# Gathered rows of the expert layer given in portions among the keys of its dense stage

## The chip, the cores and the metric

One core of a Trainium2 chip runs the whole program as one launch. The metric is the device time of the launch in microseconds, the median of several runs. The core's engines each have a queue that is worked off in order: TensorE (PE), VectorE (DVE), ScalarE (ACT), GpSimd (POOL) and SyncE (SP), which here only starts transfers.

## What is computed

A decoder block on 1024 tokens of width 1024: a time mixing and an attention run side by side and are merged, and behind them stands an expert layer. Only that layer is touched. For each token and each of 8 heads it scores 128 + 128 sub-keys, keeps the 16 best pairs, and so gets 128 expert numbers (of 16384) with a gate each:

```python
ids = (e1 * PK_NKEYS + e2).reshape(T, PK_HEADS * PK_TOPK)
gates = jax.nn.softmax(vals, axis=-1).reshape(T, PK_HEADS * PK_TOPK)
def chunk(args):                       # 128 tokens
    xc, idc, gc = args
    act = jnp.einsum('ced,cd->ce', u_tab[idc], xc)
    act = jax.nn.gelu(act, approximate=False) * gc
    return jnp.einsum('ce,ced->cd', act, v_tab[idc])
```

The sum is added to the block's input, and a last norm gives the output. All in float32.

## The kernel before

The tokens are taken in two groups of 512. For each group `mix` does the mixing part and `pick` the sub-key scores; `choose` then makes the expert numbers and gates of 128 tokens. The expert layer is done in two ways.

The first 512 tokens, four blocks of 128, go the **gathered** way (`peer`, L823). For each of the 128 chosen experts of a block, `gather` (L807) has GpSimd start an indirect transfer that brings one row of the table u for each token, 128 x 1024 numbers, into one of five buffers (tile `uv`); VectorE multiplies it with the tokens and sums (L831). Then a Gelu and the gate, and the same with 128 rows of v, which VectorE adds up with their weights (L838). `finish` (L813) squares on ScalarE, loads the weight row of the last norm, normalises on VectorE (L820) and stores. So there are 1024 gathered rows in all, each one transfer on the software queue and one VectorE operation.

The last 512 tokens go the **dense** way (`dense`, L877): all 16384 experts are worked off, 128 at a time, for all 512 tokens together. One such portion of experts is a key e, from 0 to 127. `head(e)` (L891) gets the products of the tokens with u (`dots`: two loads on SP into `wraw`, split into a high and a low part on ScalarE at L177 and VectorE at L178, 24 matmuls at L192 to L196), takes Gelu (L899), multiplies with the gates (L901, once for each key: it serves as the marker of a key below), and splits the result (`ah`, `al`, L199 and L200) and the two loaded halves of v (`vraw`, L907, to `vh` and `vl`). `add` (L912) then has 3 matmuls for each of six banks that stay in place over all keys; two more outputs are summed over two keys at a time and evicted (`rest`, L921 and L923). For the first 16 keys (NE) the products with u are made ahead, while the gates are scattered into their dense form (`gates`). At the end the banks are added (L942) and four blocks finished, with two buffers for the weight row.

The order of each engine's queue is made when the program is built: a planner goes through its own estimate of time and gives each engine the operation that is ready, the one that stands earlier in the program's text first. So text order is a rank among ready operations. In the old text the four calls of `peer` stand behind the whole of `dense`. `head(e + 1)` stands ahead of the matmuls of key e.

Of the kernel before, what the change touches and what calls it, by code (L numbers as in the profile page):

```python
# [18 lines left out]
P = 128  # L19
D = 1024  # L20
T = 1024
# [6 lines left out]
NA = 10  # L28
N4 = 4
NU = 5  # L30
ND = 4
NB = 5
NW = 3
# [15 lines left out]
def body(ctx: ExitStack, tc: tile.TileContext, ins, out, dbg=None):  # L49
# [10 lines left out]
    def zbank(name):  # L60
        return ps.tile([P, 512], F32, name=name, tag="zb", bufs=2)
# [16 lines left out]
    def at(name, dt=F32):  # L78
        return hp.tile([P, 512], dt, name=name, tag="at", bufs=NA)
# [4 lines left out]
    def t4(name):  # L84
        return hp.tile([P, D], F32, name=name, tag="t4", bufs=N4)
# [112 lines left out]
    def split(src, hi, lo):  # L198
        nc.scalar.activation(hi, src, AF.Copy)  # L199
        nc.vector.tensor_tensor(lo, src, hi.bitcast(F32), op=OP.subtract)  # L200

    def mm3(o, ah, al, bh, bl, first, last):
        nc.tensor.matmul(o, ah, bh, start=first, stop=False)  # L203
        nc.tensor.matmul(o, ah, bl, start=False, stop=False)  # L204
        nc.tensor.matmul(o, al, bh, start=False, stop=last)  # L205
# [23 lines left out]
    def normed(src, w):  # L229

        xn = [rt("xn") for _ in HALVES]
        ssq = tiny("ssq", 2)
        for i in range(2):
            nc.scalar.activation(xn[i], src[i], AF.Square, accum_out=ssq[:, i:i + 1])
        r = invroot(ssq[:, 0:1], 1, 1.0 / D, 1e-6, more=ssq[:, 1:2])
        for i in range(2):
            nc.vector.scalar_tensor_tensor(xn[i], src[i], r[:, 0:1], w[i], op0=OP.mult, op1=OP.mult)
        return xn
# [27 lines left out]
    def mix(gi, t0, W, xin=None):  # L266
# [414 lines left out]
        for a in range(TT):  # L681
# [6 lines left out]
            hn = normed(xs, nw)  # L688
            if t0 + a * P < T - ND * P:
                for i, c in enumerate(HALVES):  # L690
# [4 lines left out]
    def pick(t0, W, fh, fl):  # L695
# [5 lines left out]
        for hc in range(16):  # L701
# [12 lines left out]
            for a in range(TT):  # L714
# [7 lines left out]
                nc.vector.max_index(ix[:, 8:16], v[:, 8:16], s2)  # L722
        return [(v1[a], i1[a], t0 // P + a, t0 + a * P >= T - ND * P) for a in range(TT)]

# [82 lines left out]
    def gather(src, ids, j):  # L807
        t = pp_.tile([P, D], F32, name="uv", bufs=NU)
        nc.gpsimd.indirect_dma_start(out=t, out_offset=None, in_=ins[src],  # L809
                                     in_offset=bass.IndirectOffsetOnAxis(ap=ids[:, j:j + 1], axis=0))  # L810
        return t

    def finish(acc, rows, pool, tag, bufs):  # L813

        ssq = pool.tile([P, 1], F32, name="ssqf", bufs=2)
        fnw = pool.tile([P, D], F32, name="fnw", tag=tag, bufs=bufs)
        nc.scalar.activation(fnw, acc, AF.Square, accum_out=ssq)
        nc.sync.dma_start(fnw, ins["fnw"].to_broadcast([P, D]))
        r = invroot(ssq, 1, 1.0 / D, 1e-6, pool=pool)
        nc.vector.scalar_tensor_tensor(acc, acc, r[:, 0:1], fnw, op0=OP.mult, op1=OP.mult)  # L820
        nc.sync.dma_start(out[rows, :], acc)

    def peer(bi, ids, gate):  # L823

        rows = slice(bi * P, (bi + 1) * P)
        act = pp_.tile([P, P], F32, name="act", bufs=2)
        hb = pp_.tile([P, D], F32, name="hb", tag="ha", bufs=2)
        nc.sync.dma_start(hb, ins["hfs"][rows, :])
        for j in range(P):
            u = gather("u", ids, j)  # L830
            nc.vector.scalar_tensor_tensor(u, u, 1.0, hb, op0=OP.mult, op1=OP.mult, accum_out=act[:, j:j + 1])  # L831
        nc.scalar.activation(act, act, AF.Gelu)
        nc.vector.tensor_tensor(act, act, gate, op=OP.mult)
        acc = pp_.tile([P, D], F32, name="acc", tag="ha", bufs=2)
        nc.sync.dma_start(acc, ins["x1s"][rows, :])
        for j in range(P):
            v = gather("v", ids, j)
            nc.vector.scalar_tensor_tensor(acc, v, act[:, j:j + 1], acc, op0=OP.mult, op1=OP.add)  # L838
        finish(acc, rows, pp_, "uv", NU)

    def gates(sp, a, sl, eye8):

# [22 lines left out]
    def dots(e, W, fh, fl):  # L865
        b = zbank("ua")[:, :W]
        wmul(b, ins["ut"][e], lambda k: fh[:, k, :W], lambda k: fl[:, k, :W], step=8)
        return b
# [8 lines left out]
    def dense(t0, W, fh, fl):  # L877

        TT = W // P
        fp = ctx.enter_context(tc.tile_pool(name="fp", bufs=1))  # L880
        acc = []
        for a in range(TT):
            acc.append(t4("accd"))
            nc.sync.dma_start(acc[a], ins["x1s"][t0 + a * P:t0 + (a + 1) * P, :])
        outs = [(a, 0) for a in range(TT)] + [(a, 1) for a in range(TT)][::-1]
        banks = (rbank, rbank, rbank, obank, abank, abank)
        kept = {o: f("yk") for o, f in zip(outs, banks)}
        moved = outs[len(banks):]
        gt = [None]

        def head(e):  # L891

            if e % CE == 0:
                gt[0] = fp.tile([P, 512 // QT, CE, QT], F32, name="gt", bufs=2)
                nc.sync.dma_start(gt[0][:, :W // QT], ins["gd_s"][e // CE, :, 0:W // QT])
            w = fp.tile([P, 512], F32, name="gw", bufs=2)[:, :W]
            if e < NE:
                nc.sync.dma_start(w, ins["a_s"][e, :, 0:W])
            nc.scalar.activation(w, w if e < NE else dots(e, W, fh, fl), AF.Gelu)  # L899
            w3 = w.rearrange("p (q t) -> p q t", t=QT)  # L900
            nc.vector.tensor_tensor(w3, w3, gt[0][:, :W // QT, e % CE, :], op=OP.mult)  # L901
            v = []
            ah, al = at("ah", F32R)[:, :W], at("al", F32R)[:, :W]
            split(w, ah, al)
            for h, c in enumerate(HALVES):
                raw = fp.tile([P, 512], F32, name="vraw", bufs=NVR)
                nc.sync.dma_start(raw, ins["v"][e * P:(e + 1) * P, c])  # L907
                v.append([fp.tile([P, 512], F32R, name=n, tag=f"v{h}", bufs=NV[h]) for n in ("vh", "vl")])
                split(raw, *v[h])
            return ah, al, v  # L910

        def add(o, b, r, first, last):  # L912
            ts = slice(o[0] * P, (o[0] + 1) * P)
            mm3(b, r[0][:, ts], r[1][:, ts], *r[2][o[1]], first, last)

        def rest(o, rs):
            b = zbank("yr")
            for i, r in enumerate(rs):
                add(o, b, r, i == 0, i == CV - 1)
            t = fp.tile([P, 512], F32, name="ye", bufs=2)  # L920
            nc.scalar.activation(t, b, AF.Copy)  # L921
            y = acc[o[0]][:, HALVES[1]]
            nc.vector.tensor_tensor(y, y, t, op=OP.add)  # L923

        rs = [head(0)]
        for e in range(P):
            nxt = head(e + 1) if e + 1 < P else None
            full = rs[:CV] if e % CV == 0 and e else None
            if full:
                rs = rs[CV:]  # L930
            for n, (o, b) in enumerate(kept.items()):
                if full and n in MV:
                    rest(moved[MV.index(n)], full)
                add(o, b, rs[-1], e == 0, e == P - 1)
            rs.append(nxt)
        for o in moved:
            rest(o, rs[:CV])
        for a in range(TT):
            for h in range(2):
                if (a, h) in kept:  # L940
                    y = acc[a][:, HALVES[h]]
                    nc.vector.tensor_tensor(y, y, kept[a, h], op=OP.add)  # L942
            finish(acc[a], slice(t0 + a * P, t0 + (a + 1) * P), fp, "gt", 2)

    todo, late = [], []
# [11 lines left out]
    if "nopeer" not in dbg:  # L957
        with tc.tile_pool(name="sp", bufs=1) as sp:
            eye_f = sp.tile([P, P * 8], F32, name="eye_f", bufs=1)
            nc.sync.dma_start(eye_f, ins["eye8"])  # L960
            eye8 = sp.tile([P, P, 8], BF, name="eye8", bufs=1)
            nc.vector.tensor_copy(eye8.rearrange("p e t -> p (e t)"), eye_f)
            o = W - ND * P
            fh, fl = fh[:, :, o:W], fl[:, :, o:W]
            for a, c in enumerate(late[o // P:]):
                gates(sp, a, choose(*c), eye8)
                ahead(sp, ND * P, fh, fl, range(a * NE // ND, (a + 1) * NE // ND))
            todo += [(c[2], *choose(*c)) for c in late[:o // P]]
        dense(t0 + o, ND * P, fh, fl)
        for t in todo:  # L970
            peer(*t)


def prepare(inputs):
# [72 lines left out]
```

## Time and profile before

| | us |
|---|---|
| median of 3 runs | 3443.16 (3440.47 to 3446.24) |
| the profiled execution | 3435.12 |
| its span | 3433.4 |
| mean granted TensorE clock | 0.941 of full speed |

The profile is of one execution. Its span is what lies between the first and the last instruction; the execution is 1.7 us longer, and 8.0 us shorter than the median of the runs. Busy shares are of time; a busy DMA share is the mean of the core's 16 DMA engines.

### The profile page before, as it was taken

Reading aid. Unit: us, or ns where it says so; the run is one execution under the profiler, and the core shown is the slowest. Engines: PE = TensorE matmul, PEld = TensorE weight load, DVE = VectorE, ACT = ScalarE, POOL = GpSimd, SP = SyncE. Lnnn points to the kernel's source line nnn. Section 1 sums busy time; section 2 is a strip of 40 time slices with the busy share of each in tenths; the row PEclk is TensorE's granted clock in tenths of the full one; section 3 lists DMA queues with packets and bytes.
Section 4 is the critical chain, followed back from the end, with each engine's and each line's share of the span. In section 5 each row is a group of like instructions: output and inputs, shape, how many; then the busy total and the mean of one; then the engine's idle time right before and its main releaser. Section 6 shows DMA issues by size and latency. Waiting matters only on the chain.

```text
span 3433.4 us, 50842 instructions
## 1 busy us (share of the span) xinstructions
PE 3041.2 (89%) x17382; PEld 2379.3 (69%) x17382; DVE 2855.4 (83%) x6337; ACT 1410.6 (41%) x2632; POOL 1328.8 (39%) x1037
## 2 busy tenths in 40 slices
PE   7999998989988878798887689999998999898992
PEld 5777777766766656576565568777777777676872
DVE  5565548989898789998887689998989999889997
ACT  4444424434434423239998333333323333333331
POOL 0000000054533454212124256655655665655664
PEclk9999999999999889899988799999999999999996
DMA  4222444276666788656769999999999999999997
GB/s 135 81 77 74 140 152 161 81 253 209 216 217 222 274 322 314 204 164 187 234 202 324 333 321 353 362 348 353 355 365 350 359 354 355 360 358 350 350 327 275
DMA packets 407525, 898.68 MB, mean 262 GB/s; under 512 B 69025, under 2 KB 140001, under 8 KB 403169
## 3 DMA queue, kind: packets, MB, share of 16 engines
q0 software_dynamic: 147456, 536.94, 43.8%
q1 hardware_dynamic: 259808, 358.49, 31.2%
q8 instruction: 137, 2.24, 0.3%
q14 instruction: 124, 1.01, 0.1%
HBM read 829.22 MB, written 66.07 MB: 261 GB/s over the span
## 4 chain that ended last, share of the span: by engine, by line
issue 30%; PE 23%; POOL 18%; DVE 13%; DMA 13%; ACT 2%; POOLq 0%; SPq 0%; DVEq 0%; ACTq 0%
POOL uv L809 18%; DMA uv<-v,ids 9%; PE z L192 3%; PE z L196 3%; PE z L193 3%; DVE acc L838 2%; DMA uv<-u,ids 2%; DVE uv L831 2%; PE sc L544 1%; ACT ohg L859 1%; DVE wlo L178 1%; PE q L192 1%; PE q L196 1%; PE q L193 1%; PE oT L586 1%
## 5 line engine op out<-in xcount | busy, mean ns | idle before, releaser
L809 POOL DMA_INDIRECT uv<-u,ids x512 | 652.6, 1275 | 1226.5 <-DVE uv L831 639.4
L809 POOL DMA_INDIRECT uv<-v,ids x512 | 674.1, 1317 | 519.7 <-DVE acc L838 329.1
L838 DVE SCALAR_TENSOR_TENSOR acc<-uv,act,acc 128x1024 f32<-128x1024 f32 x512 | 655.9, 1281 | 75.7 <-DMA uv<-v,ids 70.1
L831 DVE SCALAR_TENSOR_TENSOR uv<-uv,hb 128x1024 f32<-128x1024 f32 x512 | 617.1, 1219 | 92.9 <-DMA uv<-u,ids 91.9
L177 ACT ACTIVATE whi<-wraw 128x512 fp32r<-128x512 f32 x552 | 339.8, 628 | 611.4 <-PE z L193 201.3
L178 DVE TENSOR_TENSOR wlo<-wraw,whi 128x512 fp32r<-128x512 f32 x552 | 375.0, 686 | 117.3 <-ACT whi L177 95.8
L192 PE MATMUL ua<-fh,whi 128*128 128x512 f32 x1024 | 415.9, 406 | 52.6 <-ACT ye L921 28.6
L193 PE MATMUL ua<-fl,whi 128*128 128x512 f32 x1024 | 413.3, 404 | 0.0
L199 ACT ACTIVATE ah<-gw 128x512 fp32r<-128x512 f32 x128 | 80.9, 632 | 682.4 <-DVE gw L901 682.4
L203 PE MATMUL yk<-vh,ah 128*128 128x512 f32 x768 | 308.5, 402 | 24.4 <-ACT ah L199 22.4
L205 PE MATMUL yk<-vh,al 128*128 128x512 f32 x768 | 308.4, 402 | 7.0 <-DVE al L200 6.7
L204 PE MATMUL yk<-vl,ah 128*128 128x512 f32 x768 | 304.3, 396 | 8.7 <-DVE vl L200 8.6
L196 PE MATMUL z<-hh,wlo 128*128 128x512 f32 x672 | 276.7, 412 | 6.0 <-DVE wlo L178 6.0
L192 PE MATMUL z<-hh,whi 128*128 128x512 f32 x672 | 276.6, 412 | 4.0 <-DVE carry L287 3.8
L196 PE MATMUL ua<-fh,wlo 128*128 128x512 f32 x1024 | 266.3, 398 | 15.3 <-DVE wlo L178 15.1
L193 PE MATMUL z<-hl,whi 128*128 128x512 f32 x672 | 274.6, 409 | 0.0
L192 PEld LDWEIGHTS ua<-fh,whi 128*128 128x128 f32 x1024 | 199.9, 195 | 100.2 <-ACT ye L921 32.1
L860 PE MATMUL gb<-oh,ohg 128*128 128x128 f32 x1024 | 226.4, 341 | 41.3 <-ACT ohg L859 40.4
L860 PEld LDWEIGHTS gb<-oh,ohg 128*128 128x128 f32 x1024 | 165.9, 209 | 105.2 <-ACT ohg L859 69.5
L196 PEld LDWEIGHTS ua<-fh,wlo 128*128 128x128 f32 x1024 | 193.1, 191 | 61.2 <-DVE wlo L178 22.3
L193 PEld LDWEIGHTS ua<-fl,whi 128*128 128x128 f32 x1024 | 200.0, 195 | 42.3
L859 ACT ACTIVATE ohg<-ohb,sl 128x128 f32<-128x128 bf16 x512 | 228.5, 538 | 1.8 <-DVE ohb L854 1.8
(322 smaller groups left out, 5644.7 us busy)
## 6 DMA issues: line engine op xcount, KB each, us to landing
wraw<-ut SPq DMA_DIRECT2D x256, 256.0 KB, 6.6
vraw<-v SPq DMA_DIRECT2D x256, 256.0 KB, 6.4
wraw<-w_in SPq DMA_DIRECT2D x168, 256.0 KB, 2.8
gd_s<-st SPq DMA_DIRECT2D x16, 2048.0 KB, 11.9
gt<-gd_s SPq DMA_DIRECT2D x32, 1024.0 KB, 8.9
wraw<-wq SPq DMA_DIRECT2D x64, 256.0 KB, 2.9
g_s<-sgo SPq DMA_DIRECT2D x32, 256.0 KB, 3.7
wraw<-proj SPq DMA_DIRECT2D x32, 256.0 KB, 4.1
```

Of the source, the lines that this page charges most:

```text
L177: nc.scalar.activation(hi, raw, AF.Copy)
L178: nc.vector.tensor_tensor(lo, raw, hi.bitcast(F32), op=OP.subtract)
L192: nc.tensor.matmul(o, hi, xh(k), start=(k == 0), stop=False)
L193: nc.tensor.matmul(o, hi, xl(k), start=False, stop=False)
L196: nc.tensor.matmul(o, lo, xh(k), start=False, stop=(k == n - 1))
L203: nc.tensor.matmul(o, ah, bh, start=first, stop=False)
L204: nc.tensor.matmul(o, ah, bl, start=False, stop=False)
L205: nc.tensor.matmul(o, al, bh, start=False, stop=last)
L809: nc.gpsimd.indirect_dma_start(out=t, out_offset=None, in_=ins[src], in_offset=bass.IndirectOffsetOnAxis(ap=ids[:, j:j + 1], axis=0))
L831: nc.vector.scalar_tensor_tensor(u, u, 1.0, hb, op0=OP.mult, op1=OP.mult, accum_out=act[:, j:j + 1])
L838: nc.vector.scalar_tensor_tensor(acc, v, act[:, j:j + 1], acc, op0=OP.mult, op1=OP.add)
L860: nc.tensor.matmul(b[:, k:512:4], o3[:, k], o1[:, k], start=True, stop=True)
```

## The change

`peer` becomes a generator that stops behind each gathered row. A helper `deal(n)` takes n such steps, block after block. `dense` deals 270 (NP) of them between `head(0)` and key 0, and the other 754 in even portions, one behind the matmuls of each of the 128 keys, that is 5 or 6 at a time. What is left (the last block's finish) is done behind `dense`. Operations, buffers and data are the same.

```diff
+NP = 270
...
         for j in range(P):
             u = gather("u", ids, j)
             nc.vector.scalar_tensor_tensor(u, u, 1.0, hb, op0=OP.mult, op1=OP.mult, accum_out=act[:, j:j + 1])
+            yield True
...
             nc.vector.scalar_tensor_tensor(acc, v, act[:, j:j + 1], acc, op0=OP.mult, op1=OP.add)
+            yield True
         finish(acc, rows, pp_, "uv", NU)
+
+    running = []
+
+    def deal(n):
+
+        while n:
+            if not running:
+                if not todo:
+                    return
+                running.append(peer(*todo.pop(0)))
+            if next(running[0], None):
+                n -= 1
+            else:
+                running.pop()
...
         rs = [head(0)]
+        left = 2 * P * len(todo) - NP
+        deal(NP)
         for e in range(P):
             nxt = head(e + 1) if e + 1 < P else None
...
             rs.append(nxt)
+            deal((e + 1) * left // P - e * left // P)
...
         dense(t0 + o, ND * P, fh, fl)
-        for t in todo:
-            peer(*t)
+        deal(2 * P * T)
```

## Rows read from the trace of the kernel before

**Rows 1.** Page, busy time: engine, busy us (share of the span), instructions.
```profile
PE 3041.2 (89%) x17382; PEld 2379.3 (69%) x17382; DVE 2855.4 (83%) x6337; ACT 1410.6 (41%) x2632; POOL 1328.8 (39%) x1037
```

**Rows 2.** Stretches: length; busy us of PE, PEld, DVE, ACT, POOL; PE clock, DMA share, GB/s.
```profile
1400.00:1900.00 500.00, 427.69 (x1921) 322.79 (x1920) 424.16 (x1345) 361.36 (x774) 110.22 (x95) 0.91 0.69 218
...
2031.00:3300.00 1269.00, 1194.45 (x5054) 961.45 (x5053) 1160.29 (x1609) 413.38 (x748) 767.53 (x586) 0.97 0.97 354
...
2031.60:3363.40 1331.80, 1255.49 (x5319) 1011.27 (x5317) 1217.66 (x1669) 430.92 (x778) 808.47 (x616) 0.98 0.96 352
...
2600.00:2860.00 260.00, 253.60 (x1086) 207.01 (x1085) 243.97 (x278) 90.62 (x161) 160.49 (x121) 0.98 0.98 359
2900.00:3120.00 220.00, 204.40 (x862) 162.35 (x861) 198.92 (x337) 67.98 (x126) 130.24 (x105) 0.98 0.97 356
...
3328.00:3434.00 106.00, 42.46 (x178) 33.77 (x176) 84.93 (x126) 17.18 (x30) 53.48 (x44) 0.72 0.79 276
3363.40:3434.00 70.60, 8.83 (x30) 6.46 (x30) 53.42 (x93) 8.46 (x15) 30.30 (x25) 0.58 0.77 271
...
3400.00:3410.00 10.00, 0.00 (x0) 0.00 (x0) 5.07 (x12) 0.00 (x0) 4.93 (x5) 0.50 1.02 408
```

**Rows 3.** VectorE's groups by line, 0 to 1915.8: count, busy us, mean ns, idle before.
```profile
L831 DVE SCALAR_TENSOR_TENSOR uv<-uv,hb 128x1024 f32<-128x1024 f32 x217 | 261.8, 1217 | 30.4 <-DMA uv<-u,ids 30.3
L838 DVE SCALAR_TENSOR_TENSOR acc<-uv,act,acc 128x1024 f32<-128x1024 f32 x128 | 163.8, 1279 | 15.0 <-DMA uv<-v,ids 13.9
```

**Rows 4.** The same view, keys 0 to 15 (1915.8 to 2031.6).
```profile
L831 DVE SCALAR_TENSOR_TENSOR uv<-uv,hb 128x1024 f32<-128x1024 f32 x36 | 43.3, 1220 | 3.4 <-DMA uv<-u,ids 3.4
```

**Rows 5.** The same view, keys 16 to 69 (2031.6 to 2681.4).
```profile
L838 DVE SCALAR_TENSOR_TENSOR acc<-uv,act,acc 128x1024 f32<-128x1024 f32 x166 | 212.7, 1281 | 23.8 <-DMA uv<-v,ids 21.7
L831 DVE SCALAR_TENSOR_TENSOR uv<-uv,hb 128x1024 f32<-128x1024 f32 x132 | 159.0, 1221 | 31.5 <-DMA uv<-u,ids 31.0
```

**Rows 6.** The same view, keys 70 to 126 (2681.4 to 3363.4).
```profile
L838 DVE SCALAR_TENSOR_TENSOR acc<-uv,act,acc 128x1024 f32<-128x1024 f32 x189 | 242.3, 1282 | 27.8 <-DMA uv<-v,ids 25.5
L831 DVE SCALAR_TENSOR_TENSOR uv<-uv,hb 128x1024 f32<-128x1024 f32 x128 | 154.2, 1221 | 28.4 <-DMA uv<-u,ids 28.0
```

**Rows 7.** The same view, from key 127's gate product on (3363.4 to 3434).
```profile
L838 DVE SCALAR_TENSOR_TENSOR acc<-uv,act,acc 128x1024 f32<-128x1024 f32 x30 | 38.4, 1281 | 11.3 <-DMA uv<-v,ids 11.3
```

**Rows 8.** Page, DMA queues: packets, MB, share of 16 engines; this queue carries the gathered rows.
```profile
q0 software_dynamic: 147456, 536.94, 43.8%
```

**Rows 9.** Waits of SP's queue, 2100 to 3300: us in total, times, longest.
```profile
SPq L117 <- DVE wlo L178: 616.0, 191, 10.0
...
SPq L835 <- DMA out_dram<-acc: 10.8, 2, 7.3
```

**Rows 10.** VectorE's groups by line, 3363.4 to 3390.3.
```profile
L838 DVE SCALAR_TENSOR_TENSOR acc<-uv,act,acc 128x1024 f32<-128x1024 f32 x13 | 16.7, 1281 | 6.0 <-DMA uv<-v,ids 6.0
```

**Rows 11.** Timeline of the end, VectorE, ScalarE, SP: start, us, what, idle before.
```profile
3363.43 0.68 DVE L901 TENSOR_TENSOR gw<-gw,gt 128x512 f32<-128x512 f32 x1
...
3376.00 1.29 DVE L923 TENSOR_TENSOR accd<-accd,ye 128x512 f32<-128x512 f32 x2
...
3394.26 1.28 DVE L820 SCALAR_TENSOR_TENSOR accd<-accd,rsw,fnw 128x1024 f32<-128x1024 f32 x1
...
3419.30 3.92 DVE L838 SCALAR_TENSOR_TENSOR acc<-uv,act,acc 128x1024 f32<-128x1024 f32 x3
...
3377.32 1.06 ACT L817 ACTIVATE fnw<-accd 128x1024 f32<-128x1024 f32 x1 [3.04 <-DVE accd L923]
...
3429.61 0.33 SPq L821 DMA_DIRECT2D out_dram<-acc  x1
```

**Rows 12.** The chain that ended last, one piece near the end: start, us, what.
```profile
3424.43 3.77 DMA fnw<-fnw
```

**Rows 13.** Waits of TensorE, 2640 to 3300: us in total, times, longest.
```profile
PE ua L196 <- DVE wlo L178: 6.4, 5, 2.0
```

## The prediction

> **What bounds the kernel now.** I read the page's busy shares first: TensorE and VectorE are both busy most of the span [rows 1], which tells no more than that neither average decides. The table of stretches does [rows 2]. While the gates are built (1400 to 1900) the DMA engines are 0.69 busy. From the dense stage's key 16 to its last key (2031.6 to 3363.4) they are 0.96 busy and move 352 GB/s, while PE is 94% busy and VectorE 91%. So three resources are nearly full together there, and DMA is the fullest. In the part of it that works on v rows (2600 to 2860) DMA is at 0.98 and 359 GB/s; in the part that works on u rows (2900 to 3120) at 0.97 and 356. Then comes an end of another kind: from 3328, where the last load of the dense stage is issued, DMA is 0.79 busy, and from 3363.4 on, where the last key's gate product starts (L901), PE has under 9 us of work left.
>
> Next I counted the gathered rows, with VectorE's groups cut at the keys' gate products. One gathered row is one L831 or one L838; there are 1024 (four blocks of tokens, 128 u rows and 128 v rows each). Before key 0: 217 + 128, one of them on the cut, so 344 [rows 3]. In keys 0 to 15: 36, so 380 [rows 4]. In keys 16 to 69: 298, so 678, 5.5 per key [rows 5]. In keys 70 to 126: 317, one of them on the cut, so 994, 5.5 per key [rows 6]. Behind key 127's gate product: 30 [rows 7]. These thirty are the end of the kernel: the chain of the end runs through their landings and their L838, and the dense outputs are finished in between.
>
> **The change.** No operation, no DMA and no buffer is added or removed. The gathered rows are only given to the planner earlier in the text, and thereby come before later dense work where both are ready. In the old text they stand behind the whole dense stage and fill what it leaves; that they run from far ahead of it shows that text order ranks and does not bind [rows 3].
>
> Which rows now outrank which keys: 270 are given ahead of key 0, and 754 over 128 keys, 5.89 per key. Key e's portion stands behind head(e+1) and ahead of head(e+2), so at the gate product of key k the number that outranks it is 270 + 5.89 (k - 1). Against the count above:
> - key 0 and key 16: 270 and 358 outrank, 344 and 380 are already done. The first 270 and the early portions are spent before they can push anything; I cost them at nothing. What hides them is that the planner had placed 74 more than asked by then. If the push reached back into the gates stage, DMA at 0.69 there would take a row for nothing, but the rows that could be pushed there are done.
> - key 70: 676 outrank, 678 are done. From about here the portions hold.
> - key 127: 1012 outrank, 994 are done. So 18 rows move from behind key 127's gate product to ahead of it, spread over the last 57 keys.
>
> The price of a row there: the software queue moved 536.94 MB for 1024 rows, 0.524 MB each [rows 8]; at the stretch's rate of 354 GB/s [rows 2] that is 1.48 us. VectorE's share is 1.28 us [rows 7], less than that and not added to it, since VectorE waits for rows in this stage (25.5 and 28.0 us of idle time before L838 and L831, keys 70 to 126) [rows 6]. Bounds: VectorE alone sets the pace, 18 x 1.28 = 23 us; or nothing of it, 0, if the present waits absorb the work (53.5 us are there), which I exclude as the value since those waits are for the very transfers that grow. I take 18 x 1.48 = 26.7 us: key 127's gate product moves from 3363.4 to 3390.
>
> A block's other steps move in the text with its rows: the loads of hb and acc, one Gelu, one product, and the finish of each block but the last. They issue on SP, whose queue is in order, ahead of later loads of the dense stage. Three of the four finishes lie inside the dense stage or before it today as well, and what SP waited for at such a place between 2100 and 3300 (a block's acc load behind the last block's store) was 10.8 us, while it waited 616 us for VectorE to free the buffers of the dense loads anyway [rows 9]. That slack hides them: nothing. Without it, the longest such wait, 7.3 us, would come once or twice.
>
> A rule against this change: the DMA engines in the stage move 352 to 359 GB/s, whatever the mix of u and v [rows 2]. The Trainium skill, page "DMA: Bandwidth & Descriptors", section "Where 436 GB/s comes from", gives about 358 GB/s as what one core's share of HBM allows; by it the 18 rows would cost 26.4 us as an estimate, and no order of the queues could buy them back. The trace agrees over the long stretches and not over a short one: 3400 to 3410 moved 408 GB/s [rows 2], and there the measurement decides.
>
> What follows key 127's gate product. Twelve rows are left instead of thirty. Today the first thirteen behind that point, one of them on the cut, are through by 3390.3, 26.9 us after it [rows 10]; so twelve end at 3417. The last block's own finish takes from the end of its last L838 (3423.2) to the end of the span (3433.4): 10.2 us, of which 3.77 us is the load of the weight row [rows 11, 12]. That chain ends at 3427.
>
> The dense stage's own finish is late next. From the gate product to the end of the last add of an evicted bank (L923) it is 13.9 us [rows 11]. Then four blocks are finished two at a time, because the weight row has two buffers: square (1.06 us), load (3.77), normalise (1.28), store [rows 11, 12]. With nothing in between a round is some 6.6 us from these rows, the second normalise of a round 1.2 more, the store 3.8 (from the last store's issue at 3429.6 to the end [rows 11]): 13.9 + 2 x 6.6 + 1.2 + 3.8 = 32 us, to 3422. As it runs today the first round's first normalise (L820) starts 30.8 us behind the gate product, because VectorE's queue interleaves it with gathered rows that land late [rows 11]. If the twelve rows hold the first round up as long, and the second runs free, the end is 30.8 + 2.5 + 6.6 + 3.8, some 44 us: 3434. I take 3430, between these, since twelve rows still lie over the first round but are gone by 27 us.
>
> So 3430 for the span where it is 3433.4: the rows taken from the end (about 30 us of it) are paid back nearly whole in the keys ahead of it, because DMA was already full there. The gain is only that the end's DMA share of 0.79 is entered with fewer rows. The profiled execution is 1.7 us over its span and 8.0 us under the median of the runs; with both kept, 3430 becomes 3439.8, say **3440 us**, -3.4 us. About 0.2%, 6.9 us, is what a measurement can tell from no change here.
>
> **Rivals.**
> (a) *The end closes fully and the even portions fill the DMA engines better.* For it: VectorE idles 53.5 us for rows in keys 70 to 126 [rows 6], the rate varies between 352 and 359 GB/s with the pattern [rows 2]. Against it: VectorE's queue is in order and five row buffers stay five. The price: the finish at its floor, 3422, is 11 us under today; the last 57 keys (682 us) at 359 instead of 354 GB/s give 9.5 us more. Half of the second with the first: about -16, 3427 us, faster. Under the 358 GB/s of the Trainium skill's page named above the second part would be at most 7.6 us, as an estimate.
> (b) *VectorE's queue turns the wait on PE.* A portion of six rows now stands ahead of head(e+2)'s splits (wlo at L178, ah and al at L199 and L200). Real rows land later than planned, and VectorE takes nothing out of order; so wlo comes late, and PE waits. PE waited for wlo only five times between 2640 and 3300, at most 2.0 us [rows 13]. If a wait of 2.0 us falls on one key in five of the last 57, that is 23 us: 3462, slower. It decides from five such waits more (10.3 us, the gain used up and 6.9 over).
> (c) *The change does not do what it says.* A row can be placed only when the planner thinks it landed, and only five are in flight; if that and not rank held them back, the order stays and the time is 3443.
>
> **How the numbers follow.** Chances: forecast 0.38, (a) 0.33, (b) 0.22, (c) 0.07. The forecast's bounds, 3422 and 3434 for the span, are -11 and +1; its middle and (c) lie within 0.2%. Faster 0.33, within 0.2% 0.45, slower 0.22. The range goes down to (a) with all of the finish's gain and most of the better fill (3420) and up nearly to (b)'s price (3459); the likeliest case's own is 3432 to 3446.
>
> **What would show it.** Right: keys up to about 70 at the same times as before; from there 5.9 rows per key and some 0.45 us more per key; key 127's gate product near 3390 with about 12 rows behind it; last dense store and last block's store within 10 us of each other. Wrong by (a): key 127 under 3383, or the end less than 37 us behind it. Wrong by (b): PE waits for wlo (L196 behind L178) in the last 57 keys of over 20 us in total. Wrong by (c): some 30 rows still behind key 127. My sum fails if the first 70 keys move too: then the portions reach the early stage, which I costed at nothing.

## The result: 0.75% slower, 3470 us where 3440 was forecast

The changed kernel takes 3470.03 us (median of 14 runs) against 3444.89 us for the kernel before (14 runs): ratio 1.0075, interval 1.0056 to 1.0094. The end did get shorter, as forecast; the keys ahead of it got longer by more.

| | before | after |
|---|---|---|
| span of the profiled execution | 3433.4 | 3462.8 |
| marker (gate product) of key 0 | 1915.8 | 1924.6 |
| key 0 to key 84 | 928.2 | 915.7 |
| key 84 to key 126 | 507.4 | 568.4 |
| rows in keys 84 to 126 | 235 | 245 |
| marker of key 127 to the end | 69.9 | 43.3 |
| rows behind it | 29 or 30 | 14 |

The marker is L901 before and L918 after. Two executions differ by 2 to 21 us at key 0 although next to nothing changes before it, so what follows is counted from key 0 or between keys.

Stretches of the changed kernel (columns as in [rows 2]); the first is a v stretch, the second keys 84 to 126, the third the end:

```profile
2600.00:2800.00 200.00, 194.30 (x844) 157.50 (x843) 192.85 (x222) 67.49 (x124) 122.15 (x98) 1.00 1.00 377
2840.30:3408.70 568.40, 494.25 (x2012) 388.42 (x2011) 470.57 (x675) 165.32 (x295) 291.96 (x245) 0.95 0.90 321
3419.50:3462.80 43.30, 7.39 (x33) 5.72 (x31) 35.22 (x78) 7.57 (x13) 12.88 (x10) 0.61 0.76 262
```

The same keys 84 to 126 in the kernel before:

```profile
2844.10:3351.50 507.40, 477.22 (x2026) 384.14 (x2026) 462.95 (x669) 164.00 (x295) 307.45 (x236) 0.98 0.96 348
```

In those 42 keys DMA falls from 0.96 busy and 348 GB/s to 0.90 and 321. A stage that pays for ten more rows with transfer time would show a full DMA; this one waits for something else. VectorE is busy for 7.6 us more and idle for 97.8 us instead of 44.4. Its groups there say for what. Changed kernel, keys 84 to 126 (count, busy us, mean ns, idle before and what ended it):

```profile
L832 DVE SCALAR_TENSOR_TENSOR uv<-uv,hb 128x1024 f32<-128x1024 f32 x128 | 153.3, 1222 | 10.4 <-DMA uv<-u,ids 9.4
L840 DVE SCALAR_TENSOR_TENSOR acc<-uv,act,acc 128x1024 f32<-128x1024 f32 x118 | 150.7, 1277 | 0.8 <-DMA uv<-v,ids 0.5
...
L201 DVE TENSOR_TENSOR al<-gw,ah 128x512 fp32r<-128x512 f32 x42 | 28.9, 688 | 36.4 <-ACT ah L200 36.4
L918 DVE TENSOR_TENSOR gw<-gw,gt 128x512 f32<-128x512 f32 x42 | 28.9, 687 | 46.6 <-ACT gw L916 46.6
```

The kernel before, same view, same keys (its L831 row there is the one of [rows 6]):

```profile
L838 DVE SCALAR_TENSOR_TENSOR acc<-uv,act,acc 128x1024 f32<-128x1024 f32 x108 | 138.5, 1283 | 15.3 <-DMA uv<-v,ids 14.1
...
L901 DVE TENSOR_TENSOR gw<-gw,gt 128x512 f32<-128x512 f32 x43 | 29.7, 691 | 0.0
...
L200 DVE TENSOR_TENSOR al<-gw,ah 128x512 fp32r<-128x512 f32 x42 | 28.7, 683 | 0.0
```

Before, VectorE waited almost only for rows (42 us). After, it hardly does (10 us), and waits 83 us at two places where it had not waited in these keys: for the Gelu ahead of the marker, and for ah behind it.

That it is not the rows shows best in keys 88 to 107, where all rows are u rows and the changed kernel does 113 against 112 before, and yet takes 29 us longer (before, then changed):

```profile
2891.60:3126.00 234.40, 218.80 (x926) 174.18 (x925) 210.99 (x357) 71.37 (x132) 140.32 (x113) 0.98 0.97 357
...
2892.60:3156.40 263.80, 220.48 (x886) 174.26 (x887) 213.98 (x360) 74.15 (x131) 134.29 (x114) 0.93 0.89 315
```

PE's granted clock is lower here too, 0.93 against 0.98, while PE is busy 84% of the time against 93%; what the clock adds to the loss was not separated.

PE's waits for wlo in 2860 to 3360 went from 6.4 us in 5 waits to this:

```profile
PE ua L197 <- DVE wlo L179: 62.4, 31, 11.2
```

The built program shows where that comes from. VectorE's order around keys 99 and 100 (w100: wlo of key 100; v: a split of v; G: the marker; y: an evicted bank added; a point: one gathered row):

```text
before   G99 w101 y al . v100 . y v101 v101 . . . w101 . G100 w102 . al v102 . . . . w102 w103
changed  G99 . al v99 y . . . . w100 w100 v100 v100 . G100 . al . . . . w101 w101 v101 y .
```

Before, the splits of a key stand one key to one and a half ahead of its own marker: the **lead**. In the changed kernel they stand just ahead of it, behind the rows, from key 89 on: one or two rows lie between the second split and the marker, where before it was five or six. Until key 80 or so the lead is as before, or half a key shorter for the first split; from there to key 88 it shrinks. Key 84 is where the portions begin to hold: 759 rows are done and 758 outrank.

One key of the changed kernel in order of time (start, us, what, idle before); VectorE:

```profile
3000.08 1.28 DVE L179 TENSOR_TENSOR wlo<-wraw,whi 128x512 fp32r<-128x512 f32 x2
...
3003.66 0.68 DVE L918 TENSOR_TENSOR gw<-gw,gt 128x512 f32<-128x512 f32 x1
...
3008.42 0.69 DVE L201 TENSOR_TENSOR al<-gw,ah 128x512 fp32r<-128x512 f32 x1 [2.93 <-ACT ah L200]
```

the same stretch on SP and ScalarE:

```profile
3000.79 0.93 SPq L118 DMA_DIRECT2D wraw<-ut  x2
...
3007.24 0.63 ACT L178 ACTIVATE whi<-wraw 128x512 fp32r<-128x512 f32 x1 [3.67 <-DMA wraw<-ut]
3007.78 0.61 ACT L200 ACTIVATE ah<-gw 128x512 fp32r<-128x512 f32 x1
```

The late wlo frees its load buffer at about 3000.8; only then does SP issue the next load; it lands 6 us later (6.1 in the median); ScalarE stands before its whi and has ah behind it in its queue, though the marker was done at 3004.3; so al comes at 3008.4, and VectorE, with the next rows queued behind al, stands idle for 2.9 us. This order on ScalarE, a whi between a key's Gelu and its ah, stands in keys 90 to 107 of the changed kernel and in no key of the kernel before. In the later keys (107 to 126) ah comes first again, and the wait moves to the marker: PE waits for wlo (20.9 us), the Gelu comes late, and VectorE waits 36.9 us for it.

### The profile page after: what moved, and what is told of

The parts are those of the page before. It is cut to its first block, busy times and chain, and to the rows that moved or that the text cites. A ratio compares the mean times of both kernels' runs of the same rounds, so it can differ in the third digit from the quotient of the medians.

```text
span 3462.8 us, 50655 instructions
## 1 busy us (share of the span) xinstructions
PE 3058.3 (88%) x17382; PEld 2380.5 (69%) x17382; DVE 2849.1 (82%) x6337; ACT 1411.8 (41%) x2632; POOL 1271.9 (37%) x1037
## 5 line engine op out<-in xcount | busy, mean ns | idle before, releaser
L810 POOL DMA_INDIRECT uv<-u,ids x512 | 636.8, 1244 | 1265.5 <-DVE uv L832 688.3
L810 POOL DMA_INDIRECT uv<-v,ids x512 | 633.1, 1237 | 559.1 <-DVE acc L840 413.9
L197 PE MATMUL ua<-fh,wlo 128*128 128x512 f32 x1024 | 285.6, 416 | 77.2 <-DVE wlo L179 76.9
## 6 DMA issues: line engine op xcount, KB each, us to landing
gd_s<-st SPq DMA_DIRECT2D x16, 2048.0 KB, 12.5
```

Source lines behind the costliest of these rows:

```text
L197: nc.tensor.matmul(o, lo, xh(k), start=False, stop=(k == n - 1))
```

## The experiments

Each was timed beside the kernel before on the same chip, so each ratio has its own base. The **lead theory** says that the loss is the lost lead; the rivals are that any row placed ahead of key 127 costs, or that runs of rows do.

**1. The splits of u ahead of the rows.** The changed kernel, with

```diff
+            if NE <= e + 2 < P:
+                ready.extend([wnew(ins["ut"][e + 2, i]) for i in range(2)])
             deal((e + 1) * left // P - e * left // P)
```

where `wnew` is the old `wsplit` (load and both splits) and `wsplit` takes from `ready` first.

> The changed kernel with one edit: the two loads and splits of key e+2's u half (whi, wlo) are written ahead of portion e instead of behind it; portions and rows stay. Lead theory: in the changed kernel the portions outrank the next key's splits from key 84 on, VectorE makes wlo only just in time, its load buffers come free late, the loads go out late and ScalarE and PE wait for them; that costs 1.39 us per key (59.9 us over keys 84 to 126), of which the ten extra rows explain 0.34. With the splits ahead, keys 84 to 126 go back to about 12.6 us each, the marker of key 127 comes near 3385 to 3400 and the time near 3440. Burst theory (the rival): rows in runs of four to six empty the five row buffers and leave the transfer engines idle, whatever stands between them; here the runs get longer, so the time stays at 3470 or above. Volume theory (the recorded forecast, each row costs its 1.48 us and no more): does not explain the changed kernel, and would put both at about 3437.

Measured: 3442.1 us, ratio 0.9974 (0.9953 to 0.9996). Keys 84 to 126 take 531.3 us with 244 rows, where the changed kernel takes 568.4 with 245. DMA in them (first experiment, columns as above):

```profile
2853.70:3385.00 531.30, 478.76 (x1996) 380.96 (x1997) 468.33 (x674) 165.01 (x295) 308.29 (x244) 0.97 0.95 343
```

VectorE's waits there (2860 to 3360, us in total, times, longest) for the Gelu and for ah fall from 79.5 to 10.9 us, and those for rows are back:

```profile
DVE uv L839 <- DMA uv<-u,ids: 42.0, 32, 2.7
DVE gw L925 <- ACT gw L923: 9.1, 7, 2.4
DVE acc L847 <- DMA uv<-v,ids: 5.4, 6, 1.5
DVE al L208 <- ACT ah L207: 1.8, 1, 1.8
```

With the same portions, one row less and longer runs of rows (six instead of four), 37 of the 61 us in these keys are gone, and in the total the whole loss. The rank of the two loads and splits made it. From key 0 to key 127 this version takes 13.8 us more than the kernel before for 13 more rows; the changed kernel takes 47.3 us more for 15. ScalarE still waits for late loads here (130.9 us, 118.9 in the changed kernel), so the late load by itself is not what costs. In keys 90 to 107, where ScalarE's queue ran Gelu, whi, ah, it runs Gelu, ah, whi here: the late load costs where ah, and VectorE behind it, stands behind that wait.

Not all comes back. Keys 107 to 126 take 229.8 us, 4.3 more than before with four more rows. But keys 88 to 107, with one row more than before, still take 16 us more, and VectorE waits some 37 us for u rows in them (23 before):

```profile
2905.00:3155.20 250.20, 221.42 (x913) 175.63 (x912) 210.89 (x357) 73.18 (x131) 146.05 (x113) 0.97 0.94 330
```

**2. More rows ahead of key 0.** `NP = 340`.

> The changed kernel with 340 instead of 270 rows ahead of key 0, so 5.34 per key: by the built order the splits' lead is gone in keys 14 to about 53, and is there from key 54 to the end; at key 54 40 more rows are done than in the kernel before, at key 127 29 more, none is left behind it. Volume alone: key 54's marker 59 us later than before, then 16 us won back, the end 32 us behind key 127's marker, about 3448 in all. Lead theory: 40 keys at 1.05 us on top, so key 54's marker about 100 us late and the total near 3490; from key 54 on the keys take the old 12.2 us or less although the portions still come every key.

Measured: 3481.1 us, ratio 1.0084 (1.0052 to 1.0116). Keys 16 to 54, most of them without lead, take 503.0 us instead of 455.6: 47 us more, of which seven more rows (215 against 208) explain 10 at 1.48 us; 37 us over 38 keys is 0.97 us a key, near the 1.05 taken from the changed kernel. Counted from key 0, key 54's marker is 90 us later than before, where 59 was expected from volume alone and about 100 with the lost lead. Keys 84 to 126 have their lead, and with 232 rows take 496.4 us, less than the 507.4 before, though a portion is dealt at every key. The same waits as above stand where the lead is lost (2100 to 2580):

```profile
DVE gw L918 <- ACT gw L916: 44.3, 23, 3.4
DVE al L201 <- ACT ah L200: 23.5, 12, 3.1
```

The total, 3481, is nearer to the lead theory's 3490 than to 3448. The loss goes with the lost lead and moves with it. Behind key 127's marker no row is left, and the end takes 34.7 us.

**3. Fewer rows ahead of key 0.** `NP = 200`.

> The changed kernel with 200 rows ahead of key 0, so 6.44 per key: by the built order nothing moves until key 85 or so and the splits' lead is gone only from key 107 on, 20 keys instead of 43; 13 rows are moved ahead of key 127 instead of 15. Lead theory: 13 x 1.48 + 20 x 1.05 = 40 us later at key 127, less some 27 us won behind it: near 3458, halfway between the two kernels. If the cost goes with the rows moved and not with the keys without lead, it is 13/15 of the changed kernel's: near 3466.

Measured: 3443.8 us, ratio 0.999 (0.9972 to 1.0007). Both numbers expected were missed. Sixteen rows are left behind key 127, much as in the changed kernel, yet there is no loss. The keys up to 120 run as before (18.0 us late at key 0, 18.2 at key 120) with five rows more; the last seven take 15 us more with eight rows more, and the end gives 21 us back. The lead is not gone from key 107 on, as I had expected: by the trace's order it comes and goes there, and it is lost for good only from about key 120. So few keys without lead do not part the two theories: 15 us is less than 13 rows cost at 1.48 us (19), and more than the eight rows of the last keys do (12). The outcome is near what I had forecast for the change itself: rows paid for ahead of key 127, and won back at the end.

**4. The rows in the gates stage.** The kernel before, with the dealing of `dense` taken out and, behind each quarter of the gates,

```diff
                 ahead(sp, ND * P, fh, fl, range(a * NE // ND, (a + 1) * NE // ND))
+                deal(2 * P * (a == 0) + 30)
```

> The kernel before, with the rows dealt in the gates stage instead of the dense one: 256 and 30 behind the first quarter of the gates, 30 behind each of the other three, all else behind the dense stage as before. By the built order 39 more rows are done at key 0, none is left behind key 127, and the splits' lead is that of the kernel before. Both theories: the dense stage loses 10 rows (15 us) and the end closes to about 32 us behind key 127's marker instead of 70. Open is what 39 rows cost in a stage where DMA is 0.69 and VectorE 0.85 busy: nothing to 50 us (39 x 1.28, VectorE alone). So 3392 to 3442; I take 20 us of it, 3412.

Measured: 3441.0 us, ratio 0.9984 (0.9965 to 1.0003), no change that can be told. Key 0's marker is 37 us later than in the three runs beside it, 0.95 us for each of the 39 rows; the end behind key 127 takes 33.8 us without rows. I took 20 us for it, which explains 17 of the 29 us by which 3412 was missed; the other 12 were not traced.

**5. The splits of v ahead of the rows.** The changed kernel, with `vsplit(e + 2)` (load, vh, vl) written ahead of the portion in the same way, and `whi`, `wlo` left behind it.

> The changed kernel with the v half of key e+2's splits (load, vh, vl) written ahead of portion e, and the u half (whi, wlo) left behind it. It tells what in the lost lead costs. By the built order wlo of the next key still comes after the rows and just ahead of its marker, as in the changed kernel, but between the two stand now a split and two rows in half of the keys, some 3.1 us instead of 2.4. If it is the lateness of wlo for PE that costs (PE waits 62 us for wlo in 2860 to 3360 of the changed kernel), the time stays near 3470. If it is VectorE's own wait at the marker (43 us for the Gelu, 36 us for ah, 2860 to 3360), part of it goes: about a third, near 3460. If any dense work ahead of the rows would do, as the first experiment alone might also be read, it goes to 3442.

Measured: 3456.5 us, ratio 1.0047 (1.0024 to 1.007). Keys 84 to 126 take 556.9 us, 11.5 less than the changed kernel. VectorE's waits in 2860 to 3360:

```profile
DVE gw L918 <- ACT gw L916: 23.4, 17, 3.1
...
DVE al L201 <- ACT ah L200: 15.6, 7, 3.3
```

43 and 36 us became 23 and 16; PE still waits 51.4 us for wlo. So a longer way from wlo to the marker helps a little, and it has to be the u half that goes first for the rest.

**6. Two buffers for the splits.** The kernel before with `NW = 2`.

> The kernel before with NW 2 instead of 3, two buffers for each of whi and wlo: no row's place in the text changes. By the built order 15 rows more than before are done at key 127, exactly as many as in the changed kernel, but 15 of them at key 0 already and without loss of the rank: wlo of the next key still comes one row or more before the marker of its predecessor. Lead theory: no loss per key; 15 rows less at the end; counted from key 0's marker, the time to the end is at least 10 us less than the kernel before's 1518 us (1538 in the changed kernel). If the placing of rows ahead of key 127 is itself what costs, it is near 1538. The stages before key 0 may get slower with two buffers, and that is no part of the question.

Measured: 3457.1 us, ratio 1.0045 (1.0029 to 1.0062), all of it lost ahead of key 0 (marker 41 us later than in the fifth, beside it). From key 0 the time to the end is 1496.3 us against 1517.5 before and 1538.2 in the changed kernel. It is 15 rows ahead of the kernel before at key 127, as the changed kernel is, and its keys 84 to 126 take 508.3 us with 236 rows. But those 15 rows were done ahead of key 0: between the markers of keys 0 and 127 it does 650 rows, as the kernel before does, and the changed kernel 665. So it shows that a shorter end is a gain where the dense stage has no more rows to do and its splits keep a lead of five or six rows; what more rows in that stage cost, it does not show. For that the first experiment stands.

**7 and 8. Still more rows in the gates stage.** As in the fourth, with 45 and 70 for each quarter.

> As the fourth experiment, with 45 rows for each quarter of the gates instead of 30: 81 rows more than before are done at key 0, the last row is done at key 120 and the lead is kept. 39 rows cost about 38 us in the gates stage, 0.97 us each, where a row in the dense stage costs 1.48. With the same price for 42 more, key 0's marker is 41 us later than in the fourth experiment, and the dense stage 62 us shorter: near 3420. If VectorE is full by now in the gates stage, they cost 1.28 each: 54 us, and 3433.

> The same with 70 rows for each quarter: 152 rows more than before at key 0, the last done at key 102. At 0.97 us a row it is 37 us below the run with 45 (71 rows at 0.51 gained): near 3385; at 1.28 a row 14 us below: near 3415. In the 25 keys without rows PE alone sets the pace, about 11 us a key, so part of the gain is lost there: 25 keys at 12.2 less 5.6 x 1.48 would be 3.9 us, which PE cannot do. So I expect no gain over the run with 45 rows, about the same.

Measured: 3488.4 us, ratio 1.014 (1.0112 to 1.0169), and 3610.6 us, 1.0498 (1.0471 to 1.0525). Both expectations failed. The row costs 1.33 and 1.35 us there (108 us for 81 rows, 205 for 152, against the fifth at key 0). And the dense stage gains nearly nothing: from key 0 to the end it is 1457.6 us with 45, 1459.6 with 30 and 1478.7 with 70. Up to key 84 the rows fill the gaps of every key at the same rate with 45 as with 30 (411 rows against 406). Then 16 rows are missing from keys 84 to 120, which take 10.7 us less, and 31 from the last seven keys, which take no less without any row: 75.5 us against 73.3. A row that is taken out there does not give its 1.48 us back. PE's waits for wlo in the gates stage with 45 rows (1430 to 1930) have grown as well:

```profile
PE ua L197 <- DVE wlo L179: 96.7, 4, 37.1
```

In the kernel before it is 2.1 us, and 21.7 with 30 rows. Rows that outrank a stage's own splits keep PE waiting there too.

**9. Both halves ahead of the rows,** the first and the fifth in one.

> The changed kernel with both halves of key e+2's splits ahead of portion e (the first and the fifth experiment in one). Lead theory: the first experiment took 24 us more over keys 84 to 126 than the kernel before, of which nine more rows explain 13; if the rest came from the v splits that still stood behind the rows, it goes: about 13 to 16 us over those keys, and 3432 to 3438 in all. If the rest is the price of runs of six rows in VectorE's queue, it stays: near 3442 as in the first experiment, or above it, since the runs are a little longer still.

Measured: 3454.4 us, ratio 1.0012 (0.9994 to 1.003); keys 84 to 126 take 537.5 us, no less than in the first, and the time is 12 us above that of the first experiment's kernel beside it (next). The v splits are not the rest of the loss.

**10. The first once more.**

> The first experiment's kernel once more, beside the ninth and on the same chip, to see if it is faster than the kernel before by more than the measurement is uncertain: 3442 was 0.26% below it, the interval 0.04 to 0.47%. Lead theory: again 0.1 to 0.4% below the kernel before, since the rows cost their volume and the shorter end gives it back.

Measured: 3442.0 us beside 3451.8, ratio 0.9977 (0.9963 to 0.9992); keys 84 to 126 take 530.6 us. This version is faster than both kernels: 0.23% below the one before, and by the two ratios about 1% below the changed one.

## Why the prediction was wrong

- **The bound.** Right for the kernel before, wrong as a guide: DMA, VectorE and PE are all near full in the dense stage [rows 2]. I took DMA as the price of everything there, and did not ask what the three need from each other to stay full. That is the lead. Nor was DMA at its bound: keys 54 to 84 of the changed kernel do 169 rows in 347.4 us where the kernel before does 166 in 356.9.
- **Which keys the portions reach.** Key 70 was forecast, 84 measured: the planner goes on filling gaps ahead of its quota, so the rows stayed 2 to 5 ahead of the kernel before. Keys before that cost nothing, as forecast; that they would get 12.5 us shorter was not forecast (5 to 11 us in the four runs with the same 270 rows). It is a little of what rival (a) hoped for, and it was not looked into. 15 rows moved instead of 18.
- **The price of a moved row: the step that failed.** "18 x 1.48 = 26.7 us" was to be all. From key 0 to key 127 it was 47.3 us for 15 rows, and keys 84 to 126 alone took 61.0 us more for ten more rows, 14.8 us by that price. The sum put the place where a row stands, ahead of the next key's splits, at nothing: its bounds, 0 and 23 us for VectorE, held only the work of a row. Of the 46 us that the price leaves, 37 are shown to be the lost lead, since the first experiment takes them back by rank alone; the other 9 are open. Nor is 1.48 us what a row costs where most keys keep their lead: in the first, third and tenth runs 13 more rows between the markers of keys 0 and 127 cost 13.8, 15.3 and 11.1 us.
- **The end.** 40 us behind key 127's marker was forecast (3390 to 3430), with 12 rows; 43.3 was measured, with 14. The four dense blocks' finish in two rounds is the last thing, as worked out.
- **Rival (b)** named the place (the portion ahead of the splits of head(e+2)) and the sign. Its price was too low: 2.0 us at one key in five; it was 31 waits of 2.0 us in the mean within 500 us, some 37 keys. It looked at PE alone, while the larger wait was VectorE's own, at the marker and at ah, by way of the load buffers and ScalarE's queue. I took that price from the five times that PE waited for wlo before [rows 13], and gave the rival 0.22. The few waits were the lead at work, and what the change takes away cannot be priced from how rarely it failed before. The sign I had put on record for (b), over 20 us of PE's waits for wlo, is the one that came (62.4 us).
- **The slack of SP's loads.** I wrote that SP waited 616 us for VectorE to free buffers [rows 9] and counted it as cover. It was a warning: loads that wait for wlo go out later when wlo does.
- **The rule of the Trainium skill** ("DMA: Bandwidth & Descriptors", section "Where 436 GB/s comes from", some 358 GB/s for one core): the sum did not hang on it. This case's trace differs from it: 377 GB/s over 200 us of the changed kernel, and the measurement decides.

What stays open: with the splits first, keys 84 to 126 still take 23 to 24 us more than before for nine more rows, 13 us by their transfers. But 14 to 16 us of it lie in keys 88 to 107, which do one row more than before, so the rows' transfers do not explain it. The v splits are not it; PE's waits for wlo (33.7 us against 6.4) and runs of six rows before five buffers are what is left, and neither was tried alone: the rival that runs of rows cost is refuted for the loss as a whole, not for this rest. More load buffers, which would test the way over the late loads directly, were not tried.

## What to carry to other kernels

Giving filler work a quota in the text raises its rank over all that stands later, and what loses first is the look-ahead of the main loop, not the work in hand: put the next iteration's loads and splits ahead of the portion, and count in the built order how far ahead of their use they stand, before and after, key by key where it matters. Where several engines are near full at once, a price for a moved operation has two terms, its own time and the lead that its place takes from the others; here the second was the larger, 37 us of 61 by rank alone. A wait that hardly occurs before a change shows that a margin works, not that it is spare.

## What the runs showed of the hardware that was not expected

The 16 DMA engines moved 377 GB/s over 200 us in the changed kernel (2600 to 2800, DMA share 1.00), where the kernel before moved 360 GB/s at 0.98 in the same 200 us. TensorE's work in the two is the same (844 matmuls); the changed kernel started 98 gathered rows in it instead of 93, and five rows of 0.524 MB are 13 of the 17 GB/s. I had taken 352 to 359 for full. Why more rows found room here was not looked into.
